# Second and third weight group of the first feed-forward: sums issued with the operands of p7 in place of p6

## The chip, the cores and the metric

The kernel runs on one core of a Trainium2 chip. The metric is the device time of one launch in microseconds (us). TensorE (PE in the profile) multiplies, VectorE (DVE), ScalarE (ACT) and GpSimd (POOL) prepare operands, SyncE (SP) issues the loads of weights, and GpSimd issues DMAs that add one tile to another in on-chip memory.

## What is computed

One decoder layer over 512 tokens of width 1024: a mixing block (gated MLP, block-sparse attention and a convolution side by side), cross-attention into 256 memory tokens, and a squared-ReLU MLP of hidden width 4096, each with a norm ahead and behind. The change lies in the first product of the MLP:

```python
h = rms_norm(x, pre_ffn_g[l])
f = jnp.square(jax.nn.relu(h @ w_ff1[l])) @ w_ff2[l]
x = x + rms_norm(f, post_ffn_g[l])
```

Here `h` is 512 x 1024 and `w_ff1` 1024 x 4096, both float32.

## The kernel before

**Eight groups of seven products.** The first feed-forward (`products1`) cuts `w_ff1` into eight groups of 512 columns, numbered 0 to 7 as in the code. The second and the third group of the title are groups 1 and 2. Instead of eight block products, each group makes seven (p1 to p7, after Strassen and Winograd) from four weight quarters `r[i, j]` of 128 x 1024 elements (512 KB each) and sums of them. Every product is split into three passes (high times low, high times high, low times high), so it is 24 matmuls of 128 x 256, and needs its weight operand as a pair: `fhi`, rounded by ScalarE (L113), and `flo`, the rest, by VectorE (L115).

**The sums of a group** (`Block.sums`, L901 to L914) are: t1 = r[0,0] + r[0,1] on VectorE (L907), which p5 reads; r[0,1] += r[1,1] on VectorE (L909), which p7 reads; and a DMA issued by GpSimd (L883) that adds r[0,1] to r[0,0], which p6 reads. With the operand of p6, a second DMA add puts r[0,0] onto r[1,0], which p4 reads (`Block.of`). I call these adds A and B for group 1, and C and D for group 2. Each of them waits until the one ahead has landed: B for A by its data, and D for C.

**Order of the products** (`work1`): p1 and p2 of groups 0 to 2 first (`EARLY = 3`), then (0,p5) (0,p6) (0,p3) (0,p7) (1,p5) (0,p4) (1,p6) (1,p3) (1,p7) (2,p5) (1,p4) (2,p6) and so on; from group 3 on a group has all seven in a row. `prepare1` issues the operands two products ahead (`AHEAD = 2`), and the sums of a later group hang on one of these calls. The operands of group 0's token side (`small` and `xf` tiles: p6, p3, p7, p4 in `later`, L973 to L982) are made in the same place, since every group uses them again. The tile scheduler then orders the instructions of each engine by priority, and the engines run theirs in that order.

**Buffers.** Raw quarters and t1 live in 11 buffers (`RAWS = 11`). A load into a buffer waits until the last reader of the tile that was there is done, and SyncE issues its loads in order, so a load that waits holds up all behind it. A quarter is loaded in two halves of 256 KB (L898). The loads of group 3 are the first ones that wait for what happens in group 1.

Of the kernel before, what the change touches and what calls it, by code (L numbers as in the profile page):

```python
# [35 lines left out]
def trunk(ctx: ExitStack, tc: tile.TileContext, a: dict, out: bass.AP):  # L36
# [836 lines left out]
    EARLY = 3  # L873
# [99 lines left out]
    def later(p):  # L973

        if p == 6:
            xf["n2"] = xtile()
            nc.vector.tensor_tensor(out=xf["n2"], in0=xf["n1"], in1=xf["00"], op=ALU.subtract)
        elif p == 3:
            xf["s4"] = xtile()
            nc.vector.tensor_tensor(out=xf["s4"], in0=xf["01"], in1=xf["n2"], op=ALU.add)  # L980
        split(*xo[p], xf[{6: "n2", 3: "s4", 7: "n3", 4: "11"}[p]])

    def group(n):
        def src(i, j):
            def parts(t):
                v = t.rearrange("p (b k) c -> p b k c", b=2)
                for b in range(2):
                    w = a["w_ff1"][n][2 * i + b].rearrange("p (k c) -> p k c", k=2)
                    yield v[:, b], w[:, :, j * 256:(j + 1) * 256]
            return parts  # L990
        return Block([P, 4, 256], src)
# [12 lines left out]
    def begin1():  # L1004
        for n in range(EARLY):
            blocks1[n] = group(n)
            blocks1[n].load(FIRST, ff_after[0])
        blocks1[0].load(REST, ff_after[0])
        for at in range(AHEAD):
            prepare1(at)  # L1010

    def prepare1(at):

        if at >= len(work1):
            return
        n, p = work1[at]
        if n == 0 and p in (6, 3, 7, 4):
            later(p)
        ready1[at] = blocks1[n].of(p)
        if p == 1 and n >= EARLY:  # L1020
            blocks1[n].sums(False)
        if (n, p) == (EARLY - 1, 1):
            blocks1[0].sums(True)
        if p == 6 and n + 1 < EARLY:
            blocks1[n + 1].sums(False)
        if p == 5 and n + 1 < GROUPS:
            if n + 1 >= EARLY:
                blocks1[n + 1] = group(n + 1)
                blocks1[n + 1].load(FIRST)
            blocks1[n + 1].load(REST)  # L1030

    def products1(xs):
# [40 lines left out]
        for at, (n, p) in enumerate(work):  # L1073
            if at in (1, 4):
                put_ff(xs[at // 4 + 2], at // 4 + 2)
            prepare1(at + AHEAD)
            wh, wl = ready.pop(at)
            xh, xl = xo[p]
            where = {1: "chain", 6: "chain", 7: "chain", 4: "chain", 5: "q", 3: "q", 2: "c"}[p]
            new = p in (1, 2, 5)  # L1080
            if new:
                banks[n, where] = bank()
            ps = banks[n, where]
            for f in range(2):
                c = slice(f * P, (f + 1) * P)
                for k in range(4):
                    o = ps[:, f * 256:(f + 1) * 256]
                    begin = f == 0 and k == 0 and new
                    for w, x, first_, last_ in ((wh, xl, begin, False), (wh, xh, False, False),
                                                (wl, xh, False, f == 1 and k == 3)):  # L1090
                        nc.tensor.matmul(o, lhsT=w[:, k, c], rhs=x[:, k, :], start=first_, stop=last_,  # L1091
                                         skip_group_check=True)
            out(n, p, ps)
            if p == 4 and n % 2 == 1 and n // 2 < N3S:
                m = n // 2
                x00, x10, x11 = fq[2 * m][:, :, 0:256], fq[2 * m][:, :, 256:512], fq[2 * m + 1][:, :, 256:512]
                n3s[m] = feats.tile([P, 4, 256], F32, tag="n3", name=nm("n3"), bufs=max(1, N3S))
                nc.vector.tensor_tensor(out=n3s[m], in0=x00, in1=x10, op=ALU.subtract)
                nc.vector.tensor_tensor(out=x10, in0=x10, in1=x11, op=ALU.subtract)
# [264 lines left out]
```

## Time and profile before

| | us |
|---|---|
| median of 3 runs | 712.21 (712.11 to 713.12) |
| the profiled execution: its own time | 714.04 |
| its span, first to last instruction | 712.2 |
| TensorE busy in the span | 691.1 (97%) |
| VectorE busy | 520.8 (73%) |
| ScalarE busy | 438.4 (62%) |
| GpSimd busy | 148.3 (21%) |

The first feed-forward runs from 380 us to about 515 us of the span. A row of a timeline gives start, length, engine, line, operation, tiles and count; in brackets stands the engine's idle time before it and what ended that. Names lose their buffer numbers in the trace: `in_w_ff` is `w_ff1` here, `quarter` any raw weight quarter or t1.

### The profile page before, as it was taken

The page shows a single profiled execution, that of the slowest core. Times are in us where ns is not written, and L with a number is a line of the kernel's source. Part 1 is how long each engine was busy: PE and PEld are TensorE (multiplying, and loading weights), DVE is VectorE, ACT ScalarE, POOL GpSimd, SP SyncE. Part 2 cuts the span into 40 slices and gives each one's busy share as a digit, 9 for nine tenths or more (in the row PEclk, how much of TensorE's full clock was granted, in tenths as well). Part 3 has the DMA queues.
Part 4 walks back from the last instruction along what each step waited for, and adds up shares of the span by engine and source line. Part 5 has one row for each costly group of instructions (what it writes and reads, how often), then busy time and mean ns, then how long its engine had stood idle before and what let it go on. Part 6 is the DMA issues. An engine that isn't in the chain of part 4 may idle for free.

```text
span 712.2 us, 10709 instructions
## 1 busy us (share of the span) xinstructions
PE 691.1 (97%) x4032; PEld 607.7 (85%) x4032; DVE 520.8 (73%) x773; ACT 438.4 (62%) x782; POOL 148.3 (21%) x166
## 2 busy tenths in 40 slices
PE   8999999999999999999999898999999999999994
PEld 6788888898887889888889898999999888888883
DVE  3479999977673792564468978766567888896997
ACT  6563468888794661453456856666677757656662
POOL 4545353274400110000012010000002011021311
PEclk9999999999999999999999999999999999999998
DMA  8460402243421530200165486575668879799873
GB/s 287 189 237 29 149 30 64 85 145 115 156 88 42 178 137 1 91 28 1 60 207 119 85 211 175 153 179 119 173 183 178 207 211 211 219 196 277 161 144 118
DMA packets 46132, 100.34 MB, mean 141 GB/s; under 512 B 4225, under 2 KB 21377, under 8 KB 46082
## 3 DMA queue, kind: packets, MB, share of 16 engines
q1 hardware_dynamic: 37344, 72.36, 29.7%
q0 software_dynamic: 7344, 26.74, 20.8%
q10 hardware_dynamic: 1394, 0.57, 0.4%
q8 instruction: 31, 0.51, 0.3%
q14 instruction: 19, 0.16, 0.1%
HBM read 70.83 MB, written 2.10 MB: 102 GB/s over the span
## 4 chain that ended last, share of the span: by engine, by line
PE 61%; DVE 13%; issue 10%; DMA 7%; ACT 5%; POOL 3%; SPq 1%; POOLq 0%; DVEq 0%; ACTq 0%
PE ps L124 17%; PE ps L126 17%; PE ps L125 17%; PE ps L1091 6%; DMA quarter<-quarter 4%; DMA quarter<-in_w_ff 3%; DVE flo L115 3%; POOL lo L145 2%; POOL fixed L190 1%; DVE lo L145 1%; PE ps L713 1%; DVE small L115 1%; PE ps L701 1%; DVE ps L392 1%; DVE fixed L592 1%
## 5 line engine op out<-in xcount | busy, mean ns | idle before, releaser
L1091 PE MATMUL ps<-small,fhi 128*128 128x256 f32 x896 | 162.1, 284 | 2.5 <-ACT fhi L113 1.3
L115 DVE TENSOR_TENSOR flo<-quarter,fhi 128x1024 fp32r<-128x1024 f32 x112 | 135.8, 1220 | 36.1 <-ACT fhi L113 36.0
L1091 PEld LDWEIGHTS ps<-small,fhi 128*128 128x128 f32 x896 | 139.9, 192 | 3.3 <-ACT fhi L113 1.5
L113 ACT ACTIVATE fhi<-quarter 128x1024 fp32r<-128x1024 f32 x112 | 116.0, 1053 | 33.3 <-PE ps L1091 24.5
L1091 PE MATMUL ps<-small,flo 128*128 128x256 f32 x448 | 126.9, 284 | 2.5 <-DVE flo L115 2.5
L1091 PEld LDWEIGHTS ps<-small,flo 128*128 128x128 f32 x448 | 86.0, 192 | 2.9 <-DVE flo L115 2.9
L124 PE MATMUL ps<-xl,hi 128*128 128x512 f32 (+1 forms) x256 | 87.3, 341 | 0.5 <-DVE xl L115 0.5
L124 PE MATMUL ps<-flo,small 128*128 128x512 f32 x224 | 87.6, 391 | 0.2 <-DVE flo L115 0.2
L125 PE MATMUL ps<-fhi,small 128*128 128x512 f32 x224 | 87.2, 390 | 0.0
L126 PE MATMUL ps<-fhi,small 128*128 128x512 f32 x224 | 87.2, 389 | 0.0
L125 PE MATMUL ps<-xh,hi 128*128 128x512 f32 (+1 forms) x256 | 86.2, 337 | 0.0
L126 PE MATMUL ps<-xh,lo 128*128 128x512 f32 (+1 forms) x256 | 86.2, 337 | 0.0
L883 POOL DMA_DIRECT2D quarter<-quarter x41 | 36.2, 888 | 222.7 <-DVE flo L115 92.6
L144 ACT ACTIVATE hi<-raw 128x512 fp32r<-128x512 f32 x120 | 70.1, 626 | 15.8 <-PE ps L126 11.2
L145 POOL TENSOR_TENSOR lo<-raw,hi 128x512 fp32r<-128x512 f32 x48 | 63.9, 1345 | 62.7 <-ACT hi L144 53.4
L190 POOL TENSOR_TENSOR fixed<-fixed 128x1 f32<-128x1 f32 x30 | 19.9, 664 | 236.7 <-DVE fixed L185 217.4
L145 DVE TENSOR_TENSOR lo<-raw,hi 128x512 fp32r<-128x512 f32 x72 | 52.3, 751 | 13.3 <-ACT hi L144 11.8
L124 PEld LDWEIGHTS ps<-xl,hi 128*128 128x128 f32 x256 | 48.6, 190 | 5.5 <-issue 0.7
L126 PEld LDWEIGHTS ps<-xh,lo 128*128 128x128 f32 x256 | 48.6, 190 | 5.0
L125 PEld LDWEIGHTS ps<-xh,hi 128*128 128x128 f32 x256 | 48.6, 190 | 4.7
L124 PE MATMUL ps<-lo,feat 128*128 128x512 f32 x128 | 50.6, 395 | 0.0
L124 PEld LDWEIGHTS ps<-flo,small 128*128 128x128 f32 x224 | 42.1, 188 | 10.0 <-DVE flo L115 0.7
(187 smaller groups left out, 1335.0 us busy)
## 6 DMA issues: line engine op xcount, KB each, us to landing
quarter<-quarter POOLq DMA_DIRECT2D x41, 512.0 KB, 5.1
quarter<-in_w_ff SPq DMA_DIRECT2D x64, 256.0 KB, 4.2
quarter<-in_w_ff SPq DMA_DIRECT2D x32, 512.0 KB, 5.1
raw<-in_w_xk SPq DMA_DIRECT2D x8, 512.0 KB, 3.3
raw<-in_w_xv SPq DMA_DIRECT2D x8, 512.0 KB, 4.0
raw<-in_w_out SPq DMA_DIRECT2D x8, 512.0 KB, 4.2
raw<-in_w_xq SPq DMA_DIRECT2D x8, 512.0 KB, 3.7
raw<-in_w_xo SPq DMA_DIRECT2D x8, 512.0 KB, 4.2
```

Source lines behind the costliest of these rows:

```text
L113: nc.scalar.activation(hi, src, AF.Copy, scale=1.0 if scale is None else scale)
L115: nc.vector.tensor_tensor(out=lo, in0=src, in1=hi.bitcast(F32), op=ALU.subtract)
L124: latest[0] = nc.tensor.matmul(ps, lhsT=lh, rhs=rl, start=start, stop=False, **kw)
L125: nc.tensor.matmul(ps, lhsT=lh, rhs=rh, start=False, stop=False, **kw)
L126: nc.tensor.matmul(ps, lhsT=ll, rhs=rh, start=False, stop=stop, **kw)
L144: nc.scalar.activation(hi, raw[:, c], AF.Copy)
L145: eng.tensor_tensor(out=lo, in0=raw[:, c], in1=hi.bitcast(F32), op=ALU.subtract)
L190: nc.gpsimd.tensor_tensor(out=r, in0=v, in1=neghalf[:, 0:1], op=ALU.pow)
L392: nc.vector.scalar_tensor_tensor(out=ac[:, d:], in0=y[:, 0:S - d], scalar=wdw[:, i, CONV - 1 - d:CONV - d], in1=ac[:, d:], op0=ALU.mult, o ...
L592: nc.vector.scalar_tensor_tensor(out=x_sb[:, tt, c], in0=t, scalar=r, in1=x_sb[:, tt, c], op0=ALU.mult, op1=ALU.add)
L883: nc.gpsimd.dma_start(out=out, in_=in_, accum_op=ALU.add)
L1091: nc.tensor.matmul(o, lhsT=w[:, k, c], rhs=x[:, k, :], start=first_, stop=last_, skip_group_check=True)
```

## The change

The call that issues the sums of group n + 1 (for n = 0 and n = 1) stands behind the operands of (n, p7) instead of (n, p6): two calls of `prepare1` later.

```diff
         if (n, p) == (EARLY - 1, 1):
             blocks1[0].sums(True)
-        if p == 6 and n + 1 < EARLY:
+        if p == 7 and n + 1 < EARLY:
             blocks1[n + 1].sums(False)
```

**VectorE, around the operands of (0,p3), (0,p7) and (1,p5).** Before, with flo_4247 the low part for (0,p3), flo_4280 for (0,p7), flo_4310 for (1,p5), xf_4242 the token sum for p3, small_4027 and small_4029 the low token parts for p3 and p7, and quarter_4210 and quarter_4168 the two sums of group 1:

```order
L1046 TENSOR_TENSOR fq_3119<-ps_4214,tmp_4199 128x2x256
L907 TENSOR_TENSOR quarter_4210<-quarter_3848,quarter_4168 128x1024
L980 TENSOR_TENSOR xf_4242<-xf_3879,xf_4201 128x1024
L909 TENSOR_TENSOR quarter_4168<-quarter_4168,quarter_4171 128x1024
L115 TENSOR_TENSOR flo_4247<-quarter_3863,fhi_4246 128x1024
L115 TENSOR_TENSOR small_4027<-xf_4242,small_4026 128x1024
L115 TENSOR_TENSOR flo_4280<-quarter_3860,fhi_4279 128x1024
L115 TENSOR_TENSOR small_4029<-xf_4034,small_4028 128x1024
L115 TENSOR_TENSOR flo_4310<-quarter_4210,fhi_4309 128x1024
L1046 TENSOR_TENSOR fq_3117<-ps_4250,tmp_4307 128x2x256
```

Of the change (flo_4243 is for (0,p3), flo_4276 for (0,p7), xf_4238 the token sum, quarter_4279 the first sum of group 1):

```order
L1046 TENSOR_TENSOR fq_3119<-ps_4210,tmp_4199 128x2x256
L980 TENSOR_TENSOR xf_4238<-xf_3879,xf_4201 128x1024
L115 TENSOR_TENSOR flo_4243<-quarter_3863,fhi_4242 128x1024
L907 TENSOR_TENSOR quarter_4279<-quarter_3848,quarter_4168 128x1024
L115 TENSOR_TENSOR small_4027<-xf_4238,small_4026 128x1024
L115 TENSOR_TENSOR flo_4276<-quarter_3860,fhi_4275 128x1024
L115 TENSOR_TENSOR small_4029<-xf_4034,small_4028 128x1024
L909 TENSOR_TENSOR quarter_4168<-quarter_4168,quarter_4171 128x1024
L1046 TENSOR_TENSOR fq_3117<-ps_4246,tmp_4307 128x2x256
L115 TENSOR_TENSOR flo_4310<-quarter_4279,fhi_4309 128x1024
```

The first sum moves behind the token sum of p3 (L980) and (0,p3)'s low part; the second, on which add A waits, moves behind the operands of p3 and p7. The sums of group 2 stand at the same place of VectorE's order in both programs, behind the low part of (1,p6).

**SyncE, the loads of group 3.** quarter_4479 is r[0,0], quarter_4482 r[1,0], quarter_4485 r[0,1], quarter_4488 r[1,1], each in two halves. With what each load waits for (DMASW4 is the landing of add B, DMASW3 that of add A); before:

```order
L898 DMA quarter_4479<-in_w_ff 128x2x256 [waits DMAHW5_49,DVE_49]
L898 DMA quarter_4482<-in_w_ff 128x2x256 [waits DMASW4_49,DMAHW6_49,DMASW3_49,DVE_49]
L898 DMA quarter_4485<-in_w_ff 128x2x256 [waits DMAHW7_49,PE_49]
L898 DMA quarter_4479<-in_w_ff 128x2x256 [waits DMAHW0_49]
L898 DMA quarter_4485<-in_w_ff 128x2x256 [waits DMAHW1_49]
L898 DMA quarter_4488<-in_w_ff 128x2x256 [waits DMAHW2_49,DVE_49]
```

Of the change:

```order
L898 DMA quarter_4479<-in_w_ff 128x2x256 [waits DMAHW5_49,DVE_49]
L898 DMA quarter_4482<-in_w_ff 128x2x256 [waits DMAHW6_49,PE_49]
L898 DMA quarter_4485<-in_w_ff 128x2x256 [waits DMASW4_49,DMAHW7_49,DMASW3_49,DVE_49]
L898 DMA quarter_4479<-in_w_ff 128x2x256 [waits DMAHW0_49]
L898 DMA quarter_4485<-in_w_ff 128x2x256 [waits DMAHW1_49]
L898 DMA quarter_4488<-in_w_ff 128x2x256 [waits DMAHW2_49,DVE_49]
```

The order of the loads is the same. The buffer that add B still reads goes to r[0,1] in place of r[1,0], so the queue stops for add B one load later.

**TensorE, between (0,p6) and (0,p3).** Before, two matmuls of (1,p5) (fhi_4309) stand ahead of (0,p3) (fhi_4246):

```order
L1091 MATMUL ps_3995<-small_4024,flo_4206 128x256
L1091 MATMUL ps_4388<-small_4023,fhi_4309 128x256
L1091 MATMUL ps_4388<-small_4022,fhi_4309 128x256
L1091 MATMUL ps_4250<-small_4027,fhi_4246 128x256
L1091 MATMUL ps_4250<-small_4026,fhi_4246 128x256
```

Of the change:

```order
L1091 MATMUL ps_3995<-small_4024,flo_4206 128x256
L1091 MATMUL ps_4246<-small_4027,fhi_4242 128x256
L1091 MATMUL ps_4246<-small_4026,fhi_4242 128x256
L1091 MATMUL ps_4246<-small_4026,flo_4243 128x256
L1091 MATMUL ps_4246<-small_4027,fhi_4242 128x256
```

(0,p3) follows (0,p6) directly; all of (1,p5) comes behind (0,p7). GpSimd's order is the same in both programs.

## Rows read from the trace of the kernel before

**Rows 1.** The page, TensorE's share of the span.

```profile
PE 691.1 (97%) x4032; PEld 607.7 (85%) x4032; DVE 520.8 (73%) x773; ACT 438.4 (62%) x782; POOL 148.3 (21%) x166
```

**Rows 2.** Timeline of TensorE: start, length, what, idle time before it and releaser.

```profile
404.46 0.40 PE L1091 MATMUL ps<-small,fhi 128*128 128x256 f32 x2
404.70 0.28 PE L1091 MATMUL ps<-small,flo 128*128 128x256 f32 x1
406.30 0.50 PE L1091 MATMUL ps<-small,fhi 128*128 128x256 f32 x2 [1.32 <-ACT fhi L113]
407.33 0.51 PE L1091 MATMUL ps<-small,fhi 128*128 128x256 f32 x2 [0.52 <-DVE small L115]
...
428.88 0.39 PE L1091 MATMUL ps<-small,flo 128*128 128x256 f32 x1 [1.13 <-DVE flo L115]
...
432.44 0.47 PE L1091 MATMUL ps<-small,fhi 128*128 128x256 f32 x2 [0.66 <-DVE fq L1046]
...
506.23 0.39 PE L1091 MATMUL ps<-small,flo 128*128 128x256 f32 x1 [1.32 <-DVE flo L115]
```

**Rows 3.** Timeline of VectorE, 401 to 432 us.

```profile
401.52 1.22 DVE L907 TENSOR_TENSOR quarter<-quarter,quarter 128x1024 f32<-128x1024 f32 x1
402.65 1.22 DVE L980 TENSOR_TENSOR xf<-xf,xf 128x1024 f32<-128x1024 f32 x1
403.79 1.22 DVE L909 TENSOR_TENSOR quarter<-quarter,quarter 128x1024 f32<-128x1024 f32 x1
...
406.06 1.21 DVE L115 TENSOR_TENSOR small<-xf,small 128x1024 fp32r<-128x1024 f32 x1
...
426.47 1.22 DVE L907 TENSOR_TENSOR quarter<-quarter,quarter 128x1024 f32<-128x1024 f32 x1 [5.04 <-DMA quarter<-in_w_ff]
...
431.61 0.68 DVE L1046 TENSOR_TENSOR fq<-tmp,ps 128x512 f32<-128x512 f32 x1
```

**Rows 4.** Timeline of ScalarE at the same place.

```profile
404.26 1.05 ACT L113 ACTIVATE small<-xf 128x1024 fp32r<-128x1024 f32 x1
```

**Rows 5.** Timeline of GpSimd: adds A and C are issued.

```profile
405.61 0.88 POOL L883 DMA_DIRECT2D quarter<-quarter  x1 [12.09 <-ACT small L113]
418.36 0.85 POOL L883 DMA_DIRECT2D quarter<-quarter  x1 [5.66 <-ACT fhi L113]
```

**Rows 6.** DMA adds (L883), issue to landing: all of them; add A (405 to 406 us).

```profile
DMA to landing us min/median/max: 4.5/5.4/9.8
...
DMA to landing us min/median/max: 5.6/5.6/5.6
```

**Rows 7.** The chain that ended last, 409 to 434 us: start, length, what.

```profile
411.84 4.77 DMA quarter<-quarter
...
416.75 0.54 SPq L898
...
418.65 7.63 DMA quarter<-in_w_ff
...
427.61 1.23 DVE flo L115
```

**Rows 8.** Loads (L898) to landing, issued 416.5 to 417.2 us.

```profile
DMA to landing us min/median/max: 3.3/3.3/3.3
```

**Rows 9.** DMA queues in three stretches: packets, MB, share of 16 engines (q0 adds, q1 loads).

```profile
q0 software_dynamic: 128, 0.52, 99.2%
...
q0 software_dynamic: 121, 0.49, 79.6%
q1 hardware_dynamic: 283, 0.27, 26.4%
...
q1 hardware_dynamic: 869, 0.83, 95.4%
```

These are 413 to 416 us (add B alone), 420.5 to 424 us (add C beside loads) and 424.5 to 427 us (loads, add C done).

**Rows 10.** Stretches behind the last matmul: length, PE, PEld, DVE, ACT, POOL, PEclk, DMA.

```profile
704.00:706.00 2.00, 0.00 (x0) 0.00 (x0) 1.93 (x5) 0.72 (x2) 0.55 (x1) 1.00 0.35 131
706.00:708.00 2.00, 0.00 (x0) 0.00 (x0) 1.56 (x4) 0.00 (x0) 0.93 (x1) 0.62 0.62 232
```

## What I expect, and why

> **What bounds the kernel now.** I read TensorE first: it is busy for 97% of the span [rows 1], so what counts is where it waits, and what moves those waits. The list of its waits and its timeline show four in the first feed-forward [rows 2]. Before (0,p3) it waits twice around 406 us: 1.32 us until ScalarE has rounded the weights of (1,p5), two of whose matmuls stand ahead of (0,p3), and 0.52 us until VectorE has written the low token part for p3, which ends at 407.27 [rows 2, 3]. At 428.88 it waits for the low part of (2,p5), and at 432.44 for VectorE to empty a bank. At 506 one more wait comes from the last group's loads. From 433 us on there is no other wait of over 0.2 us until the matmuls end, so a shift of TensorE behind 433 us reaches the end in full.
>
> The chain that ended last says what stands behind the wait at 428.88 [rows 7]: add B (411.84, 4.77 us), then SyncE's loads of group 3 from 416.75, the load issued at 418.65 that takes 7.63 us, then VectorE's first sum of group 3 at 426.47, for which it sat idle 5.04 us [rows 3], and only then, queued behind that sum, the low part that TensorE wants (427.61). The sum needs all halves of r[0,0] and r[0,1] of group 3. So two things hang on VectorE's queue at 402 us: the token operand for p3 at once, and, through L909, add A, add B and group 3's loads, the wait 25 us later.
>
> **What the change removes: the two sums from in front of p3's operands.** A 128 x 1024 operation takes VectorE 1.13 to 1.14 us from start to start (401.52, 402.65, 403.79) [rows 3]. By the order, L980 takes the first sum's start (401.52), (0,p3)'s low part starts at 402.65, the first sum at 403.79, the token part at 404.93 in place of 406.06. ScalarE's half of that token part started at 404.26 and takes 1.05 us [rows 4]; its source is ready 1.13 us earlier, so it ends at about 403.9, and VectorE isn't held up. (0,p3) then starts at 406.2 in place of 407.33. The two matmuls of (1,p5) that came ahead of it (0.12 us each: 0.24 from 404.46 to 404.70 for two [rows 2]) now come later. At the end of (1,p5): before 407.33 + 70 x 0.12 = 415.73, after 406.2 + 72 x 0.12 = 414.84. **Gain at this point: 0.9 us.** Of the 2.27 us that the first wait costs (404.82 to 407.33 less 0.24) 1.4 remain. The sums that moved back are hidden: (1,p5) reads the first one, and its low part is done at about 411.2, before TensorE gets to it at 412.
>
> **What it moves back: L909 and all that waits on it.** L909 goes from 403.79 to 408.33, behind two weight parts and two token parts: 4.54 us. GpSimd waits for it to issue add A; it did so 0.60 us behind L909's end (405.01 to 405.61) [rows 3, 5], so at 410.15 now. The adds are the only work in GpSimd's queue there. Add A took 5.6 us with two loads of group 2 beside it; the shortest add takes 4.5 [rows 6]. Those two loads wait for (0,p3)'s low part, now done at 403.9, and with 3.3 us for a load [rows 8] they have landed by 409. So I take 4.7: add A lands at 414.85. Add B follows 0.6 later, at 415.45. It took 4.77 us alone [rows 7]; now two loads of group 3, r[0,0] and r[1,0], of which only the second waited for add B before, run beside it, so between 4.8 and 5.6, and I take 5.2: landed at 420.65, against 416.6 before. This is 4.0 us late.
>
> SyncE then issues three loads that the first sum of group 3 needs, 0.63 us apart as in the row of before (416.75, the third behind it 418.65 with one load more) [rows 7]: 420.8, 421.4, 422.05. For the last of them the bounds are far apart: **3.3 us** if nothing is beside it [rows 8], **7.63 us** as before [rows 7]. With 0.18 us until VectorE starts (426.29 to 426.47), the sum starts between 425.5 and 429.9; before it was 426.47.
>
> Where in between is told by add C. Before, C was issued at 418.36 [rows 5], behind the first loads, and cut into the others: in 420.5 to 424 the adds' queue moved 0.49 MB at 79.6% of the engines and the loads only 0.27 MB, against 0.83 MB in the 2.5 us behind it [rows 9]; that is 0.077 MB per us beside an add and 0.33 alone. After the change C hangs on add A as well: ScalarE rounds (1,p6) when A has landed (414.85 + 1.05), VectorE's low part, first and second sum of group 2 follow (1.13 + 1.13 + 1.22), and C is issued 0.6 later, at 420.0: just ahead of the three loads instead of in their midst. An add holds the engines for about 3 us (all of 413 to 416 for add B, 0.52 MB [rows 9]) from some 1.3 us behind its issue (411.84 to 413), so 421.3 to 424.4. The loads start to move at about 422.1: 0.18 MB until 424.4. Of 0.79 MB 0.61 are left, 1.85 us at the full rate: 426.25, and half a us until the landing is told. **The sum starts at about 427.1, 0.65 us later than before.** So most of the 4 us is won back because one load fewer queues behind add B and add C no longer cuts in between.
>
> The Trainium skill (DMA: Bandwidth & Descriptors, Queues, rings and completion order) says that each DMA engine takes turns between its queues a packet at a time. Worked with the add's 128 packets [rows 9], about as many load packets of 1 KB, 0.13 MB, would pass beside it in place of 0.18, and the sum would start 0.15 us later still; the 0.27 MB of the row says more pass, so I keep the row.
>
> **The end.** TensorE arrives at (2,p5) about 0.9 us earlier and waits there until 429.5 in place of 428.88: the gain of 406 us is spent waiting. The bank at 432.44 is emptied by an operation (431.61 [rows 3]) that follows the sum in VectorE's queue without a gap, so it moves by the same 0.65. The loads of r[1,1], two more halves at 0.33 MB per us, land at about 428.4, before the second sum of group 3 at 429.4. From there on all waits are on TensorE's own progress, so the end is 0.65, say **0.7 us later**. For group 2's sums VectorE's order is unchanged and I cost that half at nothing: VectorE's other work there hides it as before, and without that cover one operation more would stand ahead of a weight part, 1.13 us. The profiled run took 714.04 us for a span of 712.2, 1.84 lying around it, and would take 714.7; the median of the runs, 712.21, goes to **712.9**.
>
> **Rivals.** *The loads are caught by an add as before* (chance 0.22): if add B lands later, near 421.1, or C's packets run on, or add D comes ahead of r[1,1]'s halves, the last load needed takes 7.63 us again, and the sum starts up to 429.9: 3.4 us late, 715.6. It is slower by over 0.2% from a start of 427.9 on. For it speaks that C and B are both tied to add A and can't drift apart; against it that C is ahead, not amid.
>
> *The loads run free* (0.12): if C is issued a us or more behind them, they land in 3.3 us, the sum starts at 425.5, TensorE resumes at 427.9 and keeps what it gained: 0.95 us less, 711.3 (710.6 if add B also took 4.5 us). C would have to lose time on VectorE that I don't see.
>
> *TensorE's clock falls in the longer wait* (0.04). It idles from about 426.6 to 429.5, 2.9 us, in place of 1.1. Behind the last matmul the granted clock was still 1.00 (2.4 GHz) in 704 to 706 us without any matmul, and 0.62 in the 2 us that follow [rows 10], so a longer idle stretch does take it to its lower level. If it fell here, the next product of 24 matmuls would take 5.8 in place of 2.9 us: 715.8. The Trainium skill (TensorE: Matmul & The Clock Gate, What's actually happening) says that the array is throttled unless recent activity releases it, and so that idle time takes the clock away; by that rule the time would be that 715.8, and the waits of 1.3 us at full clock before don't speak for it.
>
> **How the numbers follow.** The forecast has 0.62: 712.3 to 713.6, by the bounds of add B (4.8 to 5.6) and of where C starts. About 0.2%, 1.4 us, is what a measurement can tell from no change: 710.8 to 713.6. Faster by more: 0.03, the far end of free loads (710.6). Within: 0.62 and 0.09 of free loads, 0.71. Slower: 0.22 + 0.04 = 0.26. The range 711.3 to 714.8 leaves out the far half of the loads caught by an add, the clock, and the far part of the free loads, under 0.2 together.
>
> **What would show it.** (0,p3) starts at about 406.2 directly behind (0,p6); L909 at 408.3; add A at 410.1, B at 415.4, C at 420.0; the stopped load at 420.8; the first sum of group 3 at 427.1; TensorE's wait at (2,p5) grows to nearly 3 us and ends at 429.5. It is wrong if that sum starts before 426 or behind 428, or if a wait behind 433 us takes up the shift.

## The result: slower by 0.5%, and the profile after

The changed kernel takes **715.82 us** (median of 12 runs, 713.81 to 718.55) against 712.16 us: a ratio of 1.0053, 95% interval 1.0042 to 1.0064. One of the 12 runs of before, at 1381.37 us, is left out of the ratio as a slow run. I had forecast 712.9, with 711.3 to 714.8 as the range; the result is 3.7 us above before and outside it. What the first trace of the changed kernel shows comes from its fastest run, 713.81 us.

To compare two traces I lay them on the start of (0,p6), the last product that the change can't touch: it starts at 401.94 us in the trace of before and 0.78 us earlier in that of after, since the stages ahead take a little longer or shorter in each execution ((0,p6) starts between 401.1 and 403.6 us in the traces of this document). "+0.78" below means a time of after brought to before's.

The list of TensorE's waits between 400 and 510 us, by what ended them (us in total, times, longest):

```profile
PE ps L1091 <- DVE flo L115: 3.4, 1, 3.4
PE ps L1091 <- ACT small L113: 1.0, 1, 1.0
```

TensorE's timeline, which answers to [rows 2]:

```profile
405.22 0.47 PE L1091 MATMUL ps<-small,fhi 128*128 128x256 f32 x2 [1.02 <-ACT small L113]
...
425.45 0.40 PE L1091 MATMUL ps<-small,fhi 128*128 128x256 f32 x2
429.27 0.58 PE L1091 MATMUL ps<-small,flo 128*128 128x256 f32 x1 [3.42 <-DVE flo L115]
```

(0,p3) starts directly behind (0,p6), with one wait in place of two. At (2,p5) the wait is 3.42 us in place of 1.13. The waits at 432.44 and 506.23 of [rows 2] are not there.

VectorE's timeline, which answers to [rows 3]:

```profile
402.72 1.22 DVE L907 TENSOR_TENSOR quarter<-quarter,quarter 128x1024 f32<-128x1024 f32 x1
...
407.26 1.22 DVE L909 TENSOR_TENSOR quarter<-quarter,quarter 128x1024 f32<-128x1024 f32 x1
...
426.86 1.23 DVE L907 TENSOR_TENSOR quarter<-quarter,quarter 128x1024 f32<-128x1024 f32 x1 [5.06 <-DMA quarter<-in_w_ff]
428.00 1.22 DVE L115 TENSOR_TENSOR flo<-quarter,fhi 128x1024 fp32r<-128x1024 f32 x1
429.64 1.23 DVE L909 TENSOR_TENSOR quarter<-quarter,quarter 128x1024 f32<-128x1024 f32 x1 [0.43 <-DMA quarter<-in_w_ff]
...
432.52 0.68 DVE L1046 TENSOR_TENSOR fq<-tmp,ps 128x512 f32<-128x512 f32 x1
```

L909 of group 1 starts 4.25 us later than before (407.26 + 0.78 against 403.79). Group 3's first sum starts at 427.64 (+0.78) in place of 426.47, its second sum waits 0.43 us for a load, which it did not before, and the operation that empties the bank comes at 433.30 in place of 431.61: 1.7 us late.

Stretches of 2 us in the same trace: start and end, length, busy time of PE, PEld, DVE, ACT and POOL with instructions, granted clock, share of the DMA engines, GB/s:

```profile
426.00:428.00 2.00, 0.00 (x0) 0.00 (x0) 1.14 (x2) 0.00 (x0) 0.00 (x0) 1.00 1.09 348
428.00:430.00 2.00, 0.73 (x3) 0.73 (x4) 1.57 (x3) 0.00 (x0) 0.00 (x0) 0.72 1.09 240
430.00:432.00 2.00, 2.00 (x11) 2.00 (x10) 2.00 (x3) 0.49 (x1) 0.00 (x0) 0.50 0.92 242
432.00:434.00 2.00, 2.00 (x16) 1.95 (x16) 1.42 (x3) 1.97 (x4) 0.00 (x0) 0.93 0.29 96
```

Behind the wait the granted clock is 0.50, the lower of its two levels (1.2 GHz), and 11 matmuls run in 2 us where 19 do at 1.00. That is the rival to which I had given 0.04. Whether it is also the price is what the experiments had to tell.

### The profile page after: what moved, and what is told of

It is laid out like the page before. It is cut to its first block, busy times and chain, and to the rows that moved or that the text cites. A ratio compares the mean times of both kernels' runs of the same rounds, so it can differ in the third digit from the quotient of the medians.

```text
span 712.0 us, 10716 instructions
## 1 busy us (share of the span) xinstructions
PE 690.0 (97%) x4032; PEld 607.5 (85%) x4032; DVE 521.7 (73%) x773; ACT 437.9 (62%) x782; POOL 148.8 (21%) x166
## 4 chain that ended last, share of the span: by engine, by line
PE 62%; DVE 13%; DMA 9%; ACT 7%; issue 7%; POOL 2%; SPq 1%; POOLq 0%; DVEq 0%; ACTq 0%
PE ps L124 15%; PE ps L126 15%; PE ps L125 15%; PE ps L1091 12%; DMA quarter<-quarter 4%; DVE flo L115 3%; DVE lo L145 2%; DMA small<-part 1%; ACT fhi L113 1%; POOL fixed L190 1%; DMA quarter<-in_w_ff 1%; DMA tmp<-in_w_sT 1%; PE ps L713 1%; DMA fixed<-in_x 1%; PE ps L701 1%
## 5 line engine op out<-in xcount | busy, mean ns | idle before, releaser
L883 POOL DMA_DIRECT2D quarter<-quarter x41 | 36.2, 888 | 223.8 <-DVE flo L115 77.8
```

Of the source, the lines that this page charges most:

```text
L883: nc.gpsimd.dma_start(out=out, in_=in_, accum_op=ALU.add)
```

## The experiments

Each time is a median beside runs of the kernel before on the same chip.

| run | us (runs) | before (runs) | ratio, 95% |
|---|---|---|---|
| e1, changed kernel again | 715.23 (7) | 711.75 (18) | 1.0041 (1.0025 to 1.0056) |
| e2, wait filled | 715.97 (6) | 711.75 | 1.0062 (1.0048 to 1.0077) |
| e3, split first, changed kernel | 715.22 (6) | 711.75 | 1.0044 (1.0030 to 1.0059) |
| e4, split first, before | 711.34 (12) | 711.75 | 0.9992 (0.9978 to 1.0006) |
| e5, add late alone | 717.42 (6) | 712.53 (28) | 1.0066 (1.0047 to 1.0086) |
| e6, sums last, changed kernel | 715.17 (11) | 712.53 | 1.0047 (1.0027 to 1.0067) |
| e7, sums last, before | 714.51 (12) | 712.53 | 1.0028 (1.0010 to 1.0046) |
| e8, group 2's half alone | 712.71 (10) | 712.53 | 0.9997 (0.9982 to 1.0012) |
| e9, sum on GpSimd, before | 716.18 (6) | 712.02 (17) | 1.0052 (1.0032 to 1.0072) |
| e10, sum on GpSimd, changed kernel | 718.50 (5) | 712.02 | 1.0085 (1.0064 to 1.0106) |
| e11, loads past the adds | 714.11 (12) | 712.02 | 1.0036 (1.0017 to 1.0055) |
| e12, before again | 713.02 (8) | 712.40 (9) | 1.0007 (0.9988 to 1.0027) |

The second table is worked out from TensorE's timelines: how much later (us) a product starts than in the first trace of before, both laid on (0,p6). A number that stays from column to column means no wait that the first trace doesn't have. The fall of 0.8 to 1.6 us at (5,p4) in every row is that trace's own wait at 506 us. (From group 3 on p4 of a group does not stand in a row with its other products but behind p1 of the group that follows.)

| trace | (0,p7) | (1,p4) | (2,p3) | (3,p5) | (5,p1) | (5,p4) |
|---|---|---|---|---|---|---|
| e12 before again | +0.1 | -0.4 | -0.4 | -0.4 | -0.4 | -1.9 |
| e8 order of before | -0.2 | -0.8 | -0.8 | -0.8 | -0.8 | -1.5 |
| changed, first trace | -1.1 | +1.7 | +1.7 | +1.7 | +1.7 | +0.4 |
| e1 changed again | -1.2 | +2.6 | +2.9 | +2.9 | +2.9 | +1.3 |
| e2 wait filled | -1.1 | +1.8 | +1.8 | +1.8 | +2.1 | +1.1 |
| e3 split first | -1.1 | 0.0 | +2.6 | +2.6 | +2.6 | +1.3 |
| e4 split first, before | +0.1 | -1.7 | -1.7 | -1.7 | -1.7 | -3.2 |
| e5 add late alone | -0.3 | +3.6 | +3.7 | +3.7 | +3.7 | +2.3 |
| e6 sums last | -0.7 | -2.9 | -3.0 | +1.2 | +1.2 | 0.0 |
| e7 sums last, before | -0.3 | -2.5 | -2.6 | -1.1 | +1.4 | +0.5 |
| e9 GpSimd, before | -0.3 | +4.2 | +4.2 | +4.2 | +4.2 | +2.6 |
| e10 GpSimd, changed | -0.8 | +6.1 | +6.1 | +6.1 | +6.1 | +4.6 |
| e11 loads past the adds | -1.1 | -3.3 | -3.4 | -2.6 | +0.4 | -0.7 |

### e1: the changed kernel again

> The changed kernel once more, unedited, for a second trace. In the trace at hand TensorE stands idle for 3.4 us ahead of (2,p5), then runs at half its clock for some 3.3 us, which is 1.65 us of lost work; all in all the products from 433 us on are 1.8 us later against before, yet the medians differ by 3.7. Theory 1 (the wait and the clock that falls in it are the whole cost): the second trace shows a wait of 3 us or more at the same place and a granted clock of 0.5 to 0.9 in the 6 us behind it, the rest of the difference being how much longer they last in an ordinary run; median 715.8. Theory 2 (something else besides): the trace shows a second stretch in which TensorE loses 1 us or more against before, elsewhere than at (2,p5).

Its profiled run took 715.39 us, an ordinary one. The row of its wait in TensorE's timeline:

```profile
430.25 0.58 PE L1091 MATMUL ps<-small,flo 128*128 128x256 f32 x1 [3.58 <-DVE flo L115]
```

Stretches of 2 us, columns as above:

```profile
428.00:430.00 2.00, 0.00 (x0) 0.00 (x0) 2.00 (x2) 0.00 (x0) 0.00 (x0) 0.76 1.14 291
430.00:432.00 2.00, 1.75 (x8) 1.75 (x9) 1.55 (x3) 0.00 (x0) 0.00 (x0) 0.50 0.86 187
432.00:434.00 2.00, 2.00 (x11) 2.00 (x11) 2.00 (x3) 1.46 (x3) 0.00 (x0) 0.50 0.67 218
434.00:436.00 2.00, 2.00 (x12) 2.00 (x11) 1.42 (x2) 1.97 (x4) 0.00 (x0) 0.54 0.41 124
```

The wait and the fall of the clock are there again; here the lower level lasts until nearly 436 us, some 2 us longer than in the first trace, and the products are 2.9 us late in place of 1.7. No second place loses time against before. So Theory 2 falls for the changed kernel, and all of the loss is at (2,p5) and (1,p4).

### e2: the wait filled with transposes

```diff
-            ps = banks[n, where]
+            ps = banks[n, where]; _ = (n, p) == (2, 5) and fill(ps)
```

with

```python
    fill = lambda ps: [nc.tensor.transpose(out=ps[:, i % 4 * P:(i % 4 + 1) * P], in_=ident, identity=ident) for i in range(24)]
```

> The changed kernel with 24 transposes of a constant queued on TensorE right ahead of (2,p5), into the bank that (2,p5) overwrites: at 0.13 us each (8 took 1.04 us at 391.7 us of the changed kernel) they fill 3.1 us of the 3.4 us wait. Nothing else moves. Theory 1 (the clock falls because TensorE stood idle): the granted clock stays 1.00 from 426 to 434 us, the wait ahead of (2,p5) itself shrinks to 0.3 us, (2,p5) starts when it did, and its products take 2.9 us in place of some 5: the time falls by up to 1.65 us, to some 714.2. Rival (the clock falls for another cause than the idle time, say what the DMA engines draw there): the clock falls just the same and the time is 715.8 or, if the transposes at half speed outlast the wait, up to 3 us more.

TensorE's timeline (L869 are the transposes):

```profile
427.65 2.78 PE L869 MATMUL ps<-fixed 128*128 128x128 f32 x24
...
431.56 0.38 PE L1091 MATMUL ps<-small,flo 128*128 128x256 f32 x1 [0.89 <-DVE flo L115]
...
435.66 0.48 PE L1091 MATMUL ps<-small,fhi 128*128 128x256 f32 x2 [1.21 <-DVE fq L1046]
```

Stretches of 2 us, columns as above:

```profile
430.00:432.00 2.00, 1.11 (x9) 0.90 (x8) 1.55 (x3) 0.00 (x0) 0.00 (x0) 1.00 1.14 302
432.00:434.00 2.00, 2.00 (x19) 2.00 (x18) 2.00 (x3) 0.18 (x1) 0.00 (x0) 1.00 0.98 237
```

The profiled run took 717.63 us, 1.7 more than the median; most of that lies ahead of (0,p6), which starts at 403.37 us (402.01 in e1). The clock stayed at 1.00, so it does fall for TensorE's idle time and not for what the DMA engines do there. But the time did not come back: (2,p5) still starts when VectorE's low part is ready, finishes at full speed, and then TensorE waits 1.21 us for the bank that VectorE empties. (1,p4) starts 1.8 us late, as in the first trace of the changed kernel. The half-speed product was hidden: VectorE, late by the load, sets the pace. My own theory that the clock is a part of the cost falls, but for what the next lines leave.

How much it can cost: in the first trace the bank is empty at 433.30 + 0.68 = 433.98 and (1,p4) starts at 434.13, so the clock costs nothing there. In e1 the bank is empty at 434.14 and (1,p4) starts at 435.05, since (2,p5) at half speed ends only then: about 0.9 us, 1.1 by (2,p3). So 0 to 1.1 us, by how long the lower level lasts.

### e3 and e4: the low part of (2,p5) ahead of the late sum

Group 3's first sum is told to stand behind the low part of (2,p5) on VectorE:

```diff
-            nc.vector.tensor_tensor(out=self.t1, in0=r[0, 0], in1=r[0, 1], op=ALU.add)
+            not_before(nc.vector.tensor_tensor(out=self.t1, in0=r[0, 0], in1=r[0, 1], op=ALU.add), behind)
...
-            blocks1[n].sums(False)
+            blocks1[n].sums(False, lo1[2, 5] if n == 3 else None)
```

> The changed kernel with VectorE's first sum of group 3 (the one that waits for the loads) put behind the low part of (2,p5) in place of ahead of it; VectorE's order differs in this one pair. Theory 1 (the cost is all in the wait at (2,p5), and the wait is there because VectorE stands behind a load that comes late): (2,p5) starts right behind the product in front, 3.4 us earlier, the clock doesn't fall, and the time falls by up to 3.4 + 1.65 = 5 us, to some 711; what the next product then waits for (the subtraction that empties its bank stands behind the sum now) may give back 1 to 2 us of it: 711 to 713. Theory 2 (something else besides): it falls by 1.8 us at most, to 714 or above.

> The same pair exchanged in the kernel before. There the wait at (2,p5) is 1.13 us, no fall of the clock shows behind it, and another 0.66 us goes at the subtraction that empties a bank: Theory 1 expects a gain of 0.5 to 1.8 us, 710.4 to 711.7, the changed kernel with the same exchange within 1 us of it. If the exchange only moves the wait to the next product, the time stays within 0.3 us of 712.2.

TensorE's timeline in e3, its only wait of over 1.1 us in the first feed-forward:

```profile
433.21 0.77 PE L1091 MATMUL ps<-small,fhi 128*128 128x256 f32 x2 [3.16 <-DVE fq L1046]
```

The stretch behind it in e3, columns as above:

```profile
434.00:436.00 2.00, 2.00 (x11) 2.00 (x11) 0.83 (x2) 2.00 (x4) 0.00 (x0) 0.50 0.85 296
```

TensorE's timeline in e4, its longest wait between 420 and 437 us:

```profile
429.93 0.48 PE L1091 MATMUL ps<-small,fhi 128*128 128x256 f32 x2 [0.27 <-DVE fq L1046]
```

In the changed kernel the wait only goes on to the next operation behind the sum, the emptying of a bank, is 3.16 us long there, and takes the clock with it: no gain (1.0044). I had set the give-back at 1 to 2 us and it was all. In the kernel before, where the load is earlier, the trace gains 1.3 us against e12, but the medians don't separate the two (0.9992).

### e5: the late add alone

```diff
-            self.t1 = self.quarter()
-            nc.vector.tensor_tensor(out=self.t1, in0=r[0, 0], in1=r[0, 1], op=ALU.add)
-            if not by_dma:
+            if part & 1: self.t1 = self.quarter()
+            if part & 1: nc.vector.tensor_tensor(out=self.t1, in0=r[0, 0], in1=r[0, 1], op=ALU.add)
+            if not by_dma and part & 2:
...
-                dma_add(r[0, 0], r[0, 1])
+                if part & 2: dma_add(r[0, 0], r[0, 1])
...
-        if p == 6 and n + 1 < EARLY:
-            blocks1[n + 1].sums(False)
+        if p in (6, 7) and n + 1 < EARLY:
+            blocks1[n + 1].sums(False, 1 if p == 6 else 2)
```

> The kernel before, with the second sum of group 1 (L909) and the add behind it (add A) issued one product later, and the first sum left where it was: on VectorE L909 moves back by three operations, 3.4 us, and nothing else moves on any engine; the buffers of group 3's loads stay those of the kernel before. Theory 1 (the later chain of adds is the whole loss): adds A and B start 3.4 us later, the loads that wait for add B are issued some 3 us later, VectorE's first sum of group 3 ends 1 us or more later, TensorE waits 2.5 to 3.5 us ahead of (2,p5) in place of about 1.1, and without the gain ahead of (0,p3) the time is 714.5 to 716.5. Rival (the loss comes from the raw buffers, which the edit under study hands to other quarters, so that r[0,1] of group 3 now waits for add B): the time stays within 0.7 us of the kernel before, below 712.5.

Three timelines of e5: VectorE's second sum of group 1, GpSimd's issue of add A, VectorE's first sum of group 3 and TensorE's wait at (2,p5):

```profile
407.63 1.22 DVE L909 TENSOR_TENSOR quarter<-quarter,quarter 128x1024 f32<-128x1024 f32 x1
...
409.45 0.88 POOL L883 DMA_DIRECT2D quarter<-quarter  x1 [15.49 <-ACT small L113]
...
429.52 1.23 DVE L907 TENSOR_TENSOR quarter<-quarter,quarter 128x1024 f32<-128x1024 f32 x1 [5.86 <-DMA quarter<-in_w_ff]
...
431.94 0.58 PE L1091 MATMUL ps<-small,flo 128*128 128x256 f32 x1 [3.77 <-DVE flo L115]
```

This settles the cause. One VectorE operation is moved back by three places, with the buffers and the order of the loads of the kernel before (two low parts on VectorE, for (0,p3) and (0,p7), also change places; the waits at (0,p3) stay at 1.0 and 0.5 us). It makes add A 3.1 us late (this trace's (0,p6) starts 0.75 later: 408.70 against 405.61 [rows 5]) and gives all of the loss and more: 3.77 us of wait, the lower clock, and 4.9 us in the medians. The rival falls: r[0,1] of group 3 sat in the same buffer as before.

The changed kernel loses less, 3.5 to 3.7 us, though its add A goes out later, and the traces show where the difference lies. Laid on (0,p6), add B goes out at 415.46 in e5 and at 415.11 in the first trace of the changed kernel, since add A took 6.07 us to land in e5 and 4.57 there. But in e5 the queue stops for add B one load earlier, as in before, and the last load that the first sum of group 3 needs lands at 428.60 in place of 427.46; the sum starts at 428.77 in place of 427.64. The gain ahead of (0,p7) is no part of this difference, since the changed kernel spends it waiting.

### e6 and e7: the sums behind both emptying operations

The diff is that of e3, with the subtraction of (1,p7) in place of the low part (`emptied[1, 7]`).

> The changed kernel with VectorE's first sum of group 3 put behind the two subtractions that empty the banks of (1,p3) and (1,p7): three operations that TensorE waits for pass ahead of it, and the second sum follows later too. The exchange of one pair alone gained nothing, since the wait went on to the next operation behind the sum (3.2 us at the subtraction, ahead of (1,p4)). Theory 1 (what costs is only what stands behind the late loads on VectorE): no wait of over 1 us and no fall of the clock between 424 and 440 us, the products of group 2 start 3.5 to 4 us earlier than in the changed kernel, and the time is 711.0 to 711.8. Theory 2 (the late adds cost elsewhere too, at group 3's own products or at later loads): 713 or above.

> The same in the kernel before. In its trace the waits at (2,p5) and at the bank behind it are 1.13 and 0.66 us: Theory 1 expects 0.7 to 1.8 us of gain, 710.0 to 711.1. The changed kernel with the same exchange should then be faster than this one by the gain ahead of (0,p3), 1.1 us, if nothing else of the late adds costs; equal or slower if something does.

Timelines of VectorE and TensorE in e6:

```profile
439.60 1.23 DVE L907 TENSOR_TENSOR quarter<-quarter,quarter 128x1024 f32<-128x1024 f32 x1 [3.57 <-DMA quarter<-in_w_ff]
...
443.12 1.22 DVE L909 TENSOR_TENSOR quarter<-quarter,quarter 128x1024 f32<-128x1024 f32 x1 [1.16 <-DMA quarter<-in_w_ff]
...
446.82 0.47 PE L1091 MATMUL ps<-small,fhi 128*128 128x256 f32 x2 [1.91 <-DVE fq L1046]
```

The stretch behind that wait in e6, columns as above:

```profile
448.00:450.00 2.00, 2.00 (x11) 2.00 (x11) 1.09 (x2) 2.00 (x4) 0.00 (x0) 0.50 0.72 238
```

At (2,p3) both are where Theory 1 wanted them, 3 us early with no wait and a full clock. By (3,p5) and (5,p1) it is all given back: now group 4's sums stand in front of the bank, waiting for group 4's loads. Both times lie far above what Theory 1 gave; taking these products out from behind the sum gains nothing in either kernel, and the kernel before became slower by it (1.0028).

Whether the late add A costs anything beyond the waits at (2,p5) and (1,p4) is not shown by this pair. In e7 add A isn't late, and what it gives back is as much (from -2.6 to +1.4) as in e6 (from -3.0 to +1.2), so the edit itself can be the reason: on (0,p6) add D lands at 434.0 in e7 and 434.9 in e6 against 431.7 in e12, and loads of the next group go out behind it. The medians of e6 and e7 (715.17, 714.51) are not apart by more than their intervals. That the supply, adds and loads on the same DMA engines, is what runs late is how I read it, not a result of its own.

### e8: group 2's half alone

```diff
-        if p == 6 and n + 1 < EARLY:
+        if p == (7 if n == 1 else 6) and n + 1 < EARLY:
```

> Only group 2's half of the change (its sums issued at p7 of group 1, group 1's where they were). No instruction moves on any engine by it, nor do buffers change hands: all theories expect the time of the kernel before, within 0.3 us, so that the whole effect is group 1's. Its trace is a second look at the order of before: if the 1.3 us wait at 506 us of the first trace is not there, it was an accident of that execution (one add of 7.4 us), and the true difference between the kernels at 509 us is 1.3 us more than the two first traces show.

0.9997: that half does nothing, as forecast. Its trace has shorter waits than the first one of before, which led to e12.

### e9 and e10: the second sum on GpSimd

```diff
-            blocks1[n + 1].sums(False)
+            blocks1[n + 1].sums(False, nc.gpsimd if n == 0 else nc.vector)
```

> The kernel before, with the second sum of group 1 (L909) on GpSimd in place of VectorE: it starts behind L907, which ends at 402.7 us, takes some 2.7 us (GpSimd's 128x512 subtractions took 1.345 us each, twice the size here), and add A stands behind it at 405.5 to 406, where it was (405.61). VectorE is free 1.14 us earlier in front of the operands of p3 and p7. If the lateness of add A is what the change under study pays for, this keeps the chain of adds and loads in place and takes a part of the gain ahead of (0,p3) and (0,p7), 0.5 to 1.1 us: 711.0 to 711.9 against 712.2 to 712.5. Rival (the two engines slow each other down, or GpSimd's sum takes 4 us or more): add A 1.5 us or more late, and 713 to 715.

> The same in the changed kernel, where L907 itself comes 2.3 us later than in the kernel before: L909 on GpSimd from 404.8 to 407.5 (before's clock of events), add A 2 us later than in the kernel before in place of 4, the gain ahead of (0,p3) and (0,p7) of 1.1 us or more kept. With a loss in proportion to the lateness of add A (4.0 us of loss ahead of (2,p6) at 4.2 us of lateness, measured from the start of group 1's products), 2 us of loss less 1.1 to 1.5 of gain: 712.7 to 713.5. Rival (a threshold: the loss comes only when the wait is long enough for the clock to fall): 711.0 to 711.8.

GpSimd's timeline in e9:

```profile
404.27 10.07 POOL L909 TENSOR_TENSOR quarter<-quarter,quarter 128x1024 f32<-128x1024 f32 x1 [9.37 <-DMA quarter<-in_w_ff]
```

Timelines of GpSimd and TensorE in e10:

```profile
405.29 6.66 POOL L909 TENSOR_TENSOR quarter<-quarter,quarter 128x1024 f32<-128x1024 f32 x1 [11.64 <-DVE quarter L907]
...
434.71 0.58 PE L1091 MATMUL ps<-small,flo 128*128 128x256 f32 x1 [5.66 <-DVE flo L115]
```

The sum took 10.07 and 6.66 us in place of 2.7: what e9's rival had named, though its time lies above the 713 to 715 that this rival gave, and e10's lies above both of its forecasts. Add A was 7.4 and 6.6 us late (brought to (0,p6)), and the products 4.2 and 6.1. As a repair they failed. As a larger dose of lateness they agree with e5 in part: in the traces both lose more than it, by the medians only e10 does (6.5 us, against 4.9 in e5 and 4.2 in e9). The order is not that of the lateness, but it goes with the place where the queue stops: of group 3's eight loads one goes out before add B has landed in before, e5 and e10, two in the changed kernel and four in e9.

### e11: the loads past the adds

The first loads of group 3 go to r[0,0] and r[0,1], and the queue reaches the buffer that add B frees only behind them:

```diff
-                        not_before(nc.sync.dma_start(out=dst, in_=part), after)
+                        q[at] = nc.sync.dma_start(out=dst, in_=part); not_before(q[at], after)
+                        for b in behind.get(at, ()): not_before(q[at], q[b])
...
-                blocks1[n + 1].load(FIRST)
-            blocks1[n + 1].load(REST)
+                blocks1[n + 1].load(*((FIRST + REST,) if n + 1 > EARLY else G3))
+            else: blocks1[n + 1].load(REST)
```

where `G3` holds the order (0,0), (0,1), (1,0), (1,1), and (1,0) behind the first two. The second sum stands behind `emptied[1, 7]`.

> The changed kernel with group 3's loads in another order on their queue: both halves of r[0,0] and of r[0,1] into the two buffers that are free, and r[1,0], which takes the buffer that add B frees, behind them; the second sum of group 3 behind the subtractions that empty the banks. The first sum of group 3 then no longer waits for add B: it ends by 424 us in place of 429, no wait at (2,p5) nor (1,p4), no fall of the clock at 428 us. If the one stopped load were the whole loss, the time is 711.0 to 711.8. If it is the supply as a whole that is late (the adds and group 4's loads behind them), as the last two runs suggest, the waits come back at (2,p4) and (3,p5), where group 4's sums stand in front of a subtraction: 713.5 to 715.3.

TensorE's timeline, its waits of over 0.5 us between 436 and 495 us:

```profile
444.73 0.47 PE L1091 MATMUL ps<-small,fhi 128*128 128x256 f32 x2 [0.60 <-DVE fq L1046]
...
463.48 0.39 PE L1091 MATMUL ps<-small,flo 128*128 128x256 f32 x1 [1.00 <-DVE flo L115]
...
485.17 0.50 PE L1091 MATMUL ps<-small,fhi 128*128 128x256 f32 x2 [1.52 <-DVE fq L1046]
```

The waits at (2,p5) and (1,p4) are gone, and 3.8 us come back later in smaller waits, at (2,p4), (4,p1) and (5,p1). Here too add D lands late, at 433.4 on (0,p6). 1.0036 is no worse than the changed kernel, and slower than before. None of the versions is measurably faster than the kernel before.

### e12: the kernel before again

> The kernel before, unedited, for a second trace of it. Its first profiled execution took 714.04 us, 1.8 above the median of the runs beside it. Theory 1 (that execution had waits of its own, which the forecast took for the kernel's): the wait of 1.32 us at 506 us is shorter by 0.5 us or more or gone, and the waits ahead of (2,p5) and (1,p4), 1.13 and 0.66 us there, come to 1.3 us or less together. Rival (those waits are the kernel's, and ordinary runs are shorter in the stages ahead of the first feed-forward): the waits are there again and the start of (0,p6), 401.94 us in the first trace, is 1 to 2 us earlier.

TensorE's timeline, to be held against the last three of [rows 2]:

```profile
428.82 0.38 PE L1091 MATMUL ps<-small,flo 128*128 128x256 f32 x1 [0.63 <-DVE flo L115]
432.38 0.48 PE L1091 MATMUL ps<-small,fhi 128*128 128x256 f32 x2 [0.67 <-DVE fq L1046]
```

The wait at (2,p5) is half as long, and that at 506 us is gone (e8 and e4 have it shorter or not at all too); its run took 712.40 us. Theory 1: 0.4 to 0.8 us at (2,p5) and 0.8 to 1.5 us at 506 belonged to the one execution that I had read, where an add of group 5 or 6, issued at 490.03, took 7.4 us to land against 5.8 in e1.

## Why the forecast missed, step by step

**Right: the gain, and the chain of adds.** The gain ahead of (0,p7) was put at 0.9 and is 1.12 to 1.15. With 0.78 added, the trace has L909 at 408.04 (forecast 408.33), add A issued at 409.86 and landed at 414.43 (410.15, 414.85), add B from 415.11 to 420.83 (415.45, 420.65), add C at 419.84 (420.0) and the stopped load at 420.97 (420.8). Up to here each of these times is good to 0.45 us, in part by luck: add B took 5.7 us, outside of the 4.8 to 5.6 forecast, and had gone out 0.34 earlier. That group 2's half costs nothing is right as well (e8). So is the direction of "most of the 4 us is won back": add B landed 4.2 us late, the first sum of group 3 started 1.2 to 1.3 us late (1.6 to 1.7 against e12), and where one load more stands behind add B (e5) it started 2.3 us late behind an add B that was only 3.3 late.

**Wrong: how much of the 4 us is left.** Three sizes failed, all in one direction.

- *The loads beside add C.* This is the step of the sum that failed first. The forecast let 0.18 MB of loads pass while add C holds the engines, by a row of before, where the first of these loads had been issued 1.6 us ahead of C. In the changed kernel C goes out ahead of them, and hardly anything passed. The DMA queues in the first trace of the changed kernel (packets, MB, share of 16 engines; a packet's whole time counts where it starts, so that a share can exceed 100%), 420.3 to 423.2 us, then 424 to 427 us, that is 421.1 to 424.0 and 424.8 to 427.8 on (0,p6):

```profile
q0 software_dynamic: 118, 0.48, 105.6%
...
q1 hardware_dynamic: 1129, 1.09, 106.3%
q8 instruction: 1, 0.02, 2.3%
q0 software_dynamic: 4, 0.00, 0.1%
```

  The first stretch has no row for the loads (q1) at all, and neither has 421.1 to 424 us of e1's trace; the 0.13 MB that the prediction set beside its 0.18 didn't pass either. At the forecast's 0.33 MB per us 0.18 MB is 0.55 us, and the sum started at 427.64, and at 427.77 in e1, for 427.1. (The forecast's own terms add up to 426.9; its "half a us until the landing is told" stood on no row, and in the trace it is about 0.7: the 0.79 MB had gone out by some 426.8 and the last of these loads landed at 427.46. The full rate was 0.36 MB per us.)

  The third load was issued at 423.00 where I had 422.05, since SyncE's instruction for the load ahead of it was a long one. Three pieces of the chain that ended last in e2 (start, length, what), where it stands whole, to be held against the 0.54 us in [rows 7]:

```profile
423.11 1.41 SPq L898
424.52 0.04 issue
424.56 4.41 DMA quarter<-in_w_ff
```

  In the five traces of the changed order up to e6 the second and third of these loads are 1.44 to 1.47 us apart. That this delay costs anything is not shown: the DMA engines were full in both stretches above, with add C and then with loads.
- *The loads of r[1,1].* Forecast to land at 428.4, ahead of the second sum; they landed at 430.30, and VectorE, in order, waited 0.43 us (0.45 in e1). So the bank was emptied 1.7 us late and not 0.65. "So it moves by the same 0.65" is the sentence that failed here. Add D, issued at 425.79 on (0,p6), came among the last of these loads, which the prediction had only in its first rival. The queues from 428 to 430 us of the trace:

```profile
q0 software_dynamic: 91, 0.37, 93.2%
q1 hardware_dynamic: 120, 0.11, 16.0%
```

  No run moved add D, so that it makes this difference is read off the trace and not tested.
- *The base.* I read the waits of one execution of 714.04 us as those of a median of 712.21. In e12 and e8 the products from (1,p4) on are 0.4 and 0.8 us earlier than there. I had compared the times, and drawn nothing from the 1.8 us between them.

Together: 0.65 forecast, 1.0 for the loads (half of it at the first sum, half at the second), 0.4 to 0.8 for the base, and 0 to 1.1 for the clock, 2.1 to 3.6 us; the medians say 3.5 to 3.7. e1 against e12, both ordinary runs, are 3.27 us apart at (2,p3): 2.25 at the operation that empties the bank (433.46 against 431.21, on (0,p6)) and 1.0 of clock. The gain of 1.2 us is spent waiting for that operation.

**Wrong: the chance of the clock, 0.04, and its price.** It fell in both traces of the changed kernel, behind a wait of 3.4 to 3.6 us where I expected 2.9. The Trainium skill (TensorE: Matmul & The Clock Gate, What's actually happening) says that idle time takes the clock away; the trace agrees (0.50 behind 3.42 us idle, 1.00 throughout when filled), and I weighed the row of 1.3 us against it though the forecast wait was far nearer to the idle stretch of [rows 10]. The price of 2.9 us was wrong the other way: TensorE at half speed ran beside a wait for VectorE that it would have had anyhow. That 715.8 was met is no merit of that rival.

**The other rivals.** Loads caught as before: the first sum in e1 started 1.3 us late, not 3.4, so not there; but add D did come among the loads of r[1,1], at a price of half a us. Loads free: no.

**Still open.** Why SyncE's instruction takes 1.4 us there (its waits are on work long done; in before's traces a pause of the same kind, 1.6 to 1.9 us, comes behind the load that counts), why no load passed beside add C in 421 to 424 us when some did in before, and why the lower clock lasted 2 us longer in one run than in the other.

## What to carry to other kernels

An operation that starts a chain of transfers is priced by the end of the chain, where it meets the engine's own waits, and not by the place where it stands: 3.1 us of lateness at one VectorE sum cost 4.9 us in e5, in waits some 25 us later; the change gained 1.2 us on the spot. How many loads stand behind the late step counts too: with one more there, e5 lost more than the changed kernel, though its add A was less late. Where a bottleneck is a supply that several stages share, moving the waiting operation behind others gave here a local gain that the next group's operations returned in full, so compare the starts of products one after the other down to the end, not at the mended place. And before a forecast, see how far the profiled run lies from the median: 1.8 us here was a set of waits which the kernel ordinarily does not have.

## What the hardware showed that I had not expected

- GpSimd's sum of two 128x1024 tiles took 10.07 and 6.66 us beside a busy VectorE, when 128x512 took 1.345 us elsewhere in the kernel; VectorE's operations beside it kept their 1.22 us, but for the last one, in VectorE's timeline of e9:

```profile
412.58 2.83 DVE L115 TENSOR_TENSOR flo<-quarter,fhi 128x1024 fp32r<-128x1024 f32 x1
```

  The Trainium skill (SBUF — State Buffer, Who interferes with whom) says that a VectorE instruction with two inputs in SBUF contends with a GpSimd instruction that reads SBUF, and that such contention is an exclusive lock; both rows fit that.
- The clock fell behind a single wait of 1.91 us in e6 (0.50 in the stretch shown there), but not behind one of 2.24 us in e7 (1.00 throughout); so the length of one wait does not tell whether it falls. A product at half speed cost nothing where its successor waited for a bank.
